# A two-layer hybrid block: the MLP's first stage with other places for the next layer's modulation, an earlier start of its second stage, and late row sums on GpSimd

## The chip, the cores and the metric

One core of one Trainium2 chip runs the whole program: TensorE (PE, with its weight loads PEld), VectorE (DVE), ScalarE (ACT), GpSimd (POOL), and SyncE (SP), which issues all DMAs of this part. The metric is the device time of one execution in microseconds; smaller is better.

## The reference

Two layers work on a latent sequence `x` of 1024 tokens and a context of 256 tokens, width 1024. Each layer makes six modulation vectors from a conditioning vector, runs a mixer (an mLSTM with windowed attention in layer 0, full grouped attention in layer 1), and then a squared-ReLU MLP:

```python
def sq_relu_mlp(h, w1, w2):
    return jnp.square(jax.nn.relu(h @ w1)) @ w2
...
mod_l = (jax.nn.silu(c) @ ada_w[layer] + ada_b[layer]).reshape(batch, 1, N_MOD, D_MODEL)
...
x = x + mod_l[:, :, 2] * y_l
x = x + mod_l[:, :, 5] * sq_relu_mlp(modulate(x, norm2_g[layer], mod_l, 3), mlp_w1[layer], mlp_w2[layer])
if not last:
    ctx = ctx + mod_c[:, :, 5] * sq_relu_mlp(modulate(ctx, norm2_g[layer], mod_c, 3), mlp_w1[layer], mlp_w2[layer])
```

`w1` is 1024 x 4096, `w2` 4096 x 1024, and `ada_w` 1024 x 6144 per layer. The context's MLP runs in layer 0 alone.

## The kernel before

All matrix products are split into a high and a low float32r part, and each becomes three matmuls: high by high, high by low, low by high. A split is one ACT instruction (the high part, L389) and one subtraction on POOL or DVE (the low part, L390).

The MLP has two stages, and both use a Strassen-like scheme with seven products in the place of eight. **First stage** (`mlp_hidden`): 16 pairs of 128 hidden features. `pair(b, A, nxt)` is one of them for b from 2 to 15 (pairs 0 and 1 are made in `start`). It runs the seven products in this order, twelve matmuls of 128x512 each, named here by their left operand: **11, S1, 12, S2, 22, S3, S4**. In layer 0 two `direct` products for the context stand among them, one after 12 and one after S3, 24 matmuls of 128x256 each. So a pair of layer 0 takes nine PSUM banks, one after the other out of seven that rotate (`psp.tags["A"]`): the bank that product 11 of a pair writes is the one of product 12 of the pair before. What empties a bank is ACT for 11 and the direct products, and DVE (`tt`, L635) for the six others; S2 and S3 are read twice. `finish` is a ReLU and a square on ACT (L592, L593) and a store (L595). From the finished tiles DVE makes column sums (`column_sums`, three additions of two SBUF tiles) and row sums (`row_sums`, two), each with a store to DRAM (`kept_sum`, L611); a pair's row sums run in the pair after, as `pending["row"]`. The first two pairs' sums are left for later: `late_load` reads their tiles back from DRAM after pairs 7 and 10, and `late_sums` makes all five sums in pairs 8 and 11.

After some products `pair` calls `step()`, which advances `nxt`: for most pairs this is `sums(b + 1, ...)`, which makes and splits the next pair's weight operands on POOL (L553, L390) and ACT (L389), a pair ahead. In pair 15 there is no next pair, and `nxt` is `ahead()`: it loads and splits the first three items (k = 0, 1, 2) of the **second stage** (`mlp_feed`, `mlp_out`), each of which has a weight part `a` and a hidden part `b` (`load_a`, `load_b`, L915; `split_a` with an addition on POOL, L960; `split_b`). The raw tiles of `a` lie in three places of the buffer F that the first stage's weights used; those of `b` lie in two more, which the scratch tile of `sums` and the filler's tiles below occupy until then. From the fourth item (k = 3) on, `feed.more()` loads into the buffers of the normalised input, which are free after the last product of the first stage, and splits on DVE.

In layer 0 a **filler** goes along: `ada_sums(1, block, ...)` makes the next layer's modulation, twelve blocks of 512 outputs. Each block loads eight chunks of `ada_w` (128x512, L204) and adds them up on DVE, scaled per partition (L211, L213); blocks 0 to 3 do it for latent and context, with two more instructions of 128x256 per chunk. Then 8 or 16 small matmuls against ones (L222) sum over the partitions, and DVE adds the bias (L225). It is a generator with three steps per block: chunks 0 to 3, chunks 4 to 7, and the matmuls with the bias. `fill(k)` in `pair` runs one step if b > k, at three places per pair.

Pairs 2 to 13 are ordered by the framework's planner: it works through the traced program with a cost model and can move an instruction of one engine ahead of others; program order is its priority. Pairs 14 and 15 stand in a `manual_schedule` block: there PE, DVE, ACT, POOL and SP keep the order in which the program is written. On every engine, and in SP's queue of DMA issues, an instruction that waits holds up all that stand behind it.

The second stage (L1037) takes per item 24 matmuls of 128x512 from four banks each of two output halves; items 0 and 1 are taken together, in four works of twelve: item 0, item 1, item 0, item 1.

Of the kernel before, what the change touches and what calls it, by code (L numbers as in the profile page):

```python
# [10 lines left out]
F32 = mybir.dt.float32  # L11
# [3 lines left out]
ALU = mybir.AluOpType  # L15
# [4 lines left out]
P = 128  # L20
# [76 lines left out]
class Kernel:  # L97
# [96 lines left out]
            nc.vector.tensor_tensor(dst[:, :, :, vv], src[:, :, :, vv], bias, op=ALU.add)  # L194
        yield

    def ada_sums(self, layer, block, streams, tp, psp, tag):


        nc, a = self.nc, self.a  # L200
        acc = [[tp.tile([P, n], F32, tag=f"acc{v}") for _ in range(512 // n)] for v, n in enumerate((512, 256)[:streams])]
        for k in range(ND):
            w = tp.tile([P, 512], F32, tag="raw")
            nc.sync.dma_start(w, a["ada_w"][layer, k * P : (k + 1) * P, block * 512 : block * 512 + 512])  # L204
            for v in range(streams):
                c = self.cs[:, k, v : v + 1]
                n = 512 // len(acc[v])
                for i, t in enumerate(acc[v]):
                    x = w[:, i * n : i * n + n]
                    if k == 0:  # L210
                        nc.vector.tensor_scalar(t, x, c, None, op0=ALU.mult)  # L211
                    else:
                        nc.vector.scalar_tensor_tensor(t, x, c, t, op0=ALU.mult, op1=ALU.add)  # L213
            if k % 4 == 3:
                yield
        pt = psp.tile(tag, "adapt")
        for v in range(streams):
            n = 4 // len(acc[v])
            for i in range(4):
                o = 8 * v + 2 * i  # L220
                t = acc[v][i // n][:, i % n * P : i % n * P + P]
                nc.tensor.matmul(pt[:, o : o + 2], t, self.ones[:, 0:2], start=True, stop=True)  # L222
        c0 = block * 4
        for v in range(streams):
            nc.vector.tensor_tensor(  # L225
                self.mod[layer][:, c0 : c0 + 4, v], pt[:, 8 * v : 8 * v + 8].rearrange("p (i e) -> p i e", e=2)[:, :, 0],
                self.v(V_AB + layer * 48 + c0, 4), op=ALU.add,
            )
        yield

    def ada_quarter(self, q, tp, psp):

# [273 lines left out]
    def mlp_hidden(self, layer, groups, hds, begin, slots, tp, feed, filler):  # L506
# [80 lines left out]
        def temp(n=512):  # L587
            return tp.tile([P, n], F32, tag="u")
# [20 lines left out]
        def kept_sum(b, i, o, p, q, how=ALU.add):  # L609
            tt(o, p, q, how)  # L610
            nc.sync.dma_start(part(b, i), o)  # L611

        def late_load(b):

            h = [temp() for _ in range(4)]
            for t, i in zip(h, (5, 7, 8, 2)):
                nc.sync.dma_start(t, part(b, i))

            def late_sums():
                column_sums(b, h[0], h[2], h[3])  # L620
                row_sums(b, h[0], h[1], h[3])

            return late_sums

# [2 lines left out]
            kept_sum(b, 0, temp(), h11, h22)  # L627
            kept_sum(b, 4, h21, h21, h22)

        def row_sums(b, h11, h12, h22):  # L630
            kept_sum(b, 6, temp(), h12, h22, ALU.subtract)
            kept_sum(b, 3, h12, h11, h12)

        def tt(o, p, q, how=ALU.add):
            nc.vector.tensor_tensor(o, p, q, op=how)  # L635
# [150 lines left out]
        def pair(b, A, nxt):  # L786
# [62 lines left out]
        def ahead():  # L849


            at = tp.tags["op"][1]
            w = W[slots[5]]
            tp.place("op", [parts[(at + i) % 10] for i in range(10)] + [w[:, :PG], w[:, PG:]])
            tp.place("raw", cuts(F, PG, 0, PG, 2 * PG))
            tp.place("b", cuts(F, PG, 5 * PG, 6 * PG))
            eng = nc.gpsimd
            if filler:
                yield
                yield  # L860
            for k in range(2):
                feed.load(k)
            feed.load_a(2)
            yield
            feed.split_a(0, eng)
            yield
            feed.split_b(0, eng)
            feed.load_b(2)
# [1440 lines left out]
def body(ctx: ExitStack, tc: tile.TileContext, a, out):  # L2309
# [68 lines left out]
    def filler(tp, psp, tag):  # L2378
        if not steps:

            steps.append(s for b in range(12) for s in k.ada_sums(1, b, 2 if b < 4 else 1, tp, psp, tag))
        return steps[0]

    def to_mixer1(g, psp, gap):
# [30 lines left out]
```

## Time and profile before

| | |
|---|---|
| median of 3 runs | 2825.57 us (2825.43 to 2827.79) |
| the profiled execution | 2826.91 us; its span from first to last instruction is 2825.1 us |
| PE busy | 2716.9 us (96%) |
| DVE, ACT, POOL busy | 1953.8 (69%), 1474.9 (52%), 1114.1 us (39%) |
| granted TensorE clock, mean | 0.986 |
| first stage, pairs 2 to 15: layer 0, layer 1 | about 840 to 1231 us, about 2238 to 2504 us |
| second stage begins: layer 0, layer 1 | about 1231 us, about 2504 us |

Times in the profile are microseconds from the first instruction. A busy PE is not PE at its peak, since a matmul's record overlaps the next one's; what tells a loss is idle time before a matmul and the granted clock. In a row of the timeline the bracket at the end is the idle time of that engine just before the instruction, and what ended it. In the view by stretches, each engine's column is its busy time in the stretch, with the number of instructions, and the last three columns are the granted clock, the DMA engines' busy share and the rate.

### The profile page before, as it was taken

How to read it: one execution, taken by the hardware profiler on the slowest of the kernel's cores; microseconds unless marked ns; L12 is line 12 of the kernel's file. 1: busy time of each engine (PE TensorE's matmuls, PEld its weight loads, DVE VectorE, ACT ScalarE, POOL GpSimd, SP SyncE). 2: the span in 40 equal slices, each digit the busy share in tenths (PEclk: the TensorE clock that was granted, in tenths of full speed). 3: DMA queues.
4: the chain of work that ended last, by engine and by line, in shares of the span. 5: the costliest groups of instructions: out<-in, count | busy, mean ns of one | idle time of the engine just before them, and what ended most of it. 6: DMA issues, size and time to landing. Idle time of an engine off the chain costs nothing.

```text
span 2825.1 us, 40958 instructions
## 1 busy us (share of the span) xinstructions
PE 2716.9 (96%) x14747; PEld 2303.2 (82%) x14747; DVE 1953.8 (69%) x3299; ACT 1474.9 (52%) x2611; POOL 1114.1 (39%) x741
## 2 busy tenths in 40 slices
PE   6899999999999999989999999999999999999999
PEld 3788888878788887868888889999988888878877
DVE  4645555578878877667778756888874667666676
ACT  4755554444664343334346646888865555444442
POOL 2421121111238565630001346777775398740000
PEclk9999999999999999999999999999999999999999
DMA  7222233442325567578856820000036155477674
GB/s 238 66 78 94 94 101 137 142 162 87 119 84 154 179 214 233 167 251 304 282 182 193 254 68 25 22 27 20 27 119 215 58 172 199 166 269 261 220 228 153
DMA packets 194661, 428.36 MB, mean 152 GB/s; under 512 B 21128, under 2 KB 47336, under 8 KB 194456
## 3 DMA queue, kind: packets, MB, share of 16 engines
q1 hardware_dynamic: 194456, 425.73, 45.7%
q8 instruction: 116, 1.90, 0.3%
q14 instruction: 89, 0.73, 0.1%
HBM read 322.90 MB, written 102.74 MB: 151 GB/s over the span
## 4 chain that ended last, share of the span: by engine, by line
PE 61%; DVE 12%; DMA 6%; issue 5%; ACT 3%; POOL 3%; SPq 0%; DVEq 0%; POOLq 0%; ACTq 0%
PE psum L1037 16%; PE psum L580 11%; PE psum L415 4%; PE psum L417 4%; PE psum L416 4%; PE psum L2003 4%; PE psum L2189 3%; PE psum L1133 3%; DMA hhiraw<-in_w 3%; PE psum L1909 3%; DVE F L635 2%; POOL W L390 2%; DVE W L390 2%; DVE x L213 1%; DVE F L213 1%
## 5 line engine op out<-in xcount | busy, mean ns | idle before, releaser
L390 POOL TENSOR_TENSOR W<-F,W 128x512 fp32r<-128x512 f32 (+2 forms) x323 | 518.0, 1619 | 546.9 <-ACT W L389 430.0
L1037 PE MATMUL psum<-W,W 128*128 128x512 f32 x2688 | 620.2, 393 | 14.9 <-POOL W L390 8.3
L1037 PEld LDWEIGHTS psum<-W,W 128*128 128x128 f32 x2688 | 507.1, 189 | 127.7 <-POOL W L390 10.1
L580 PE MATMUL psum<-hhi,W 128*128 128x512 f32 (+1 forms) x1600 | 450.1, 361 | 10.2 <-DVE x L635 8.3
L389 ACT ACTIVATE W<-F 128x512 fp32r<-128x512 f32 (+2 forms) x380 | 273.4, 739 | 263.8 <-POOL F L553 97.7
L580 PEld LDWEIGHTS psum<-hhi,W 128*128 128x128 f32 x1600 | 290.0, 192 | 56.8 <-DVE x L635 8.0
L580 PE MATMUL psum<-hlo,W 128*128 128x512 f32 (+1 forms) x800 | 287.9, 360 | 0.0
L389 ACT ACTIVATE W<-hhiraw 128x1024 fp32r<-128x1024 f32 x98 | 103.8, 1060 | 308.6 <-PE psum L1037 204.2
L415 PE MATMUL psum<-hhi,W 128*128 128x512 f32 (+1 forms) x624 | 233.4, 374 | 0.5 <-ACT F L1422 0.5
L417 PE MATMUL psum<-hhi,W 128*128 128x512 f32 (+1 forms) x624 | 227.0, 364 | 0.0
L416 PE MATMUL psum<-hlo,W 128*128 128x512 f32 (+1 forms) x624 | 226.6, 363 | 0.0
L553 POOL TENSOR_TENSOR F<-F 128x512 f32<-128x512 f32 x112 | 167.5, 1496 | 19.4 <-DMA F<-in_w 10.8
L960 DVE TENSOR_TENSOR hhiraw<-hhiraw 128x512 f32<-128x512 f32 x154 | 106.2, 701 | 98.2 <-DMA hhiraw<-in_w 97.4
L580 PEld LDWEIGHTS psum<-hlo,W 128*128 128x128 f32 x800 | 154.0, 192 | 21.6 <-issue 0.2
L390 DVE TENSOR_TENSOR W<-hhiraw,W 128x1024 fp32r<-128x1024 f32 x98 | 119.7, 1222 | 64.9 <-ACT W L389 63.6
L382 POOL TENSOR_TENSOR hlo<-F,hhi 128x512 fp32r<-128x512 f32 (+1 forms) x24 | 27.4, 1144 | 342.4 <-ACT F L373 342.4
L415 PEld LDWEIGHTS psum<-hhi,W 128*128 128x128 f32 x624 | 118.2, 189 | 21.0 <-ACT x L389 2.5
L416 PEld LDWEIGHTS psum<-hlo,W 128*128 128x128 f32 x624 | 118.4, 190 | 17.3 <-issue 2.2
L417 PEld LDWEIGHTS psum<-hhi,W 128*128 128x128 f32 x624 | 118.1, 189 | 17.0 <-issue 0.2
L390 DVE TENSOR_TENSOR W<-hloraw,W 128x1024 fp32r<-128x1024 f32 x98 | 119.6, 1220 | 6.8 <-ACT W L389 6.8
L592 ACT ACTIVATE F<-F 128x512 f32<-128x512 f32 x82 | 51.3, 626 | 139.5 <-DVE F L635 139.5
L580 PE MATMUL psum<-x,W 128*128 128x512 f32 x504 | 123.5, 389 | 0.0
(442 smaller groups left out, 6367.6 us busy)
## 6 DMA issues: line engine op xcount, KB each, us to landing
F<-in_w SPq DMA_DIRECT2D x104, 512.0 KB
hloraw<-hd SPq DMA_DIRECT2D x90, 512.0 KB
hhiraw<-in_w SPq DMA_DIRECT2D x72, 512.0 KB
hd<-F SPq DMA_DIRECT2D x142, 256.0 KB
hhiraw<-in_w SPq DMA_DIRECT2D x116, 256.0 KB
F<-in_ada_w SPq DMA_DIRECT2D x96, 256.0 KB
hd<-x SPq DMA_DIRECT2D x90, 256.0 KB
F<-in_win SPq DMA_DIRECT2D x33, 512.0 KB
```

What stands on the lines that cost most here:

```text
L389: nc.scalar.activation(hi, src, AF.Copy)
L390: eng.tensor_tensor(lo, src, hi.bitcast(F32), op=ALU.subtract)
L415: nc.tensor.matmul(ps, sh, mh, start=i == 0, stop=False)
L416: nc.tensor.matmul(ps, sh, ml, start=False, stop=False)
L417: nc.tensor.matmul(ps, sl, mh, start=False, stop=i == n - 1)
L553: add = lambda o, p, q, how: nc.gpsimd.tensor_tensor(o, p, q, op=how)
L580: nc.tensor.matmul(ps, w[i][:, p], B[j][k], start=first and j == 0 and m == 0, stop=last and j == 3 and m == 2)
L960: tt = lambda o, p, q, how: eng.tensor_tensor(o, p, q, op=how)
L1037: nc.tensor.matmul(bank(base + i), A[u][:, p], B[v], start=first and m == 0, stop=last and m == 2)
L1133: nc.tensor.matmul(bank(k), B[u][:, i * P : i * P + P], A[v][:, half], start=f == 0 and m == 0, stop=f == NFF - 1 and m == 2,)
L1909: nc.tensor.matmul(ps, s[:, c], m[:, j, t0 : t0 + QT], start=j == 0 and i == 0, stop=j == ND - 1 and i == 2)
L2003: nc.tensor.matmul(u.o[:, :QT], v[x], p[y], start=c == 0 and m == 0, stop=c == 2 * NB - 1 and m == 2)
```

## The change

Five edits, in both layers unless said otherwise:

1. `ada_sums` takes all twelve blocks in one generator and keeps up to three chunk loads ahead, also over the end of a step or of a block: `load()` runs before each chunk and again just before a step ends. The tiles are the same three as before.
2. The filler's steps move in `pair` (layer 0): the first two from around the reading of product 12 to behind the two readings of S2, the third from behind 22 to behind the readings of S3.
3. In `ahead`, layer 0 begins two steps earlier, and in both layers loads and splits are interleaved: loads of a0, b0, a1 after product 11; split a0 after S1; split b0 and the load of a2 after 12; the load of b1 and split a1 after S2; the load of b2 after 22; split b1 after S3; splits a2 and b2 after S4. Layer 1 loaded a0, b0, a1, b1 and a2 after product 11 before, and split a1 and b1 both after S3.
4. The raw places of `a` in the second stage begin with the third of the three.
5. `late_sums` makes its two row sums on POOL in the place of DVE: two instructions in pair 8 and two in pair 11 of each layer.

```diff
+    def ada_sums(self, layer, blocks, tp, psp, tag):
...
+        todo = deque((block, k) for block, _ in blocks for k in range(ND))
+        ready = deque()
+        def load():
+            while todo and len(ready) < 3:
+                block, k = todo.popleft()
+                ready.append(tp.tile([P, 512], F32, tag="raw"))
+                src = a["ada_w"][layer, k * P : (k + 1) * P, block * 512 : block * 512 + 512]
+                nc.sync.dma_start(ready[-1], src)
...
         for k in range(ND):
-            w = tp.tile([P, 512], F32, tag="raw")
-            nc.sync.dma_start(w, a["ada_w"][layer, k * P : (k + 1) * P, block * 512 : block * 512 + 512])
+                load()
+                w = ready.popleft()
...
-            if k % 4 == 3:
-                yield
+                if k % 4 == 3:
+                    load()
+                    yield
...
-                row_sums(b, h[0], h[1], h[3])
+                row_sums(b, h[0], h[1], h[3], nc.gpsimd)
...
             prod(ps, A["12"], B21)
-            fill(3)
             tt(h11, ps, t)
             finish(h11, h11, part(b, 5))
-            fill(2)
...
             prod(ps, A["S2"], T2)
             tt(v, ps, v)
             tt(t, ps, t)
+            fill(3)
+            fill(2)
             step()
             ps = bank()
             prod(ps, A["22"], T4)
             tt(t, t, ps, ALU.subtract)
-            fill(2)
             step()
             ps = bank()
             prod(ps, A["S3"], T3)
...
             finish(t, t)
             finish(h22, h22, part(b, 2))
+            fill(2)
...
-            tp.place("raw", cuts(F, PG, 0, PG, 2 * PG))
+            tp.place("raw", cuts(F, PG, 2 * PG, 0, PG))
...
-            if filler:
-                yield
-                yield
-            for k in range(2):
-                feed.load(k)
+            feed.load(0)
+            feed.load_a(1)
+            yield
+            feed.split_a(0, eng)
+            yield
+            feed.split_b(0, eng)
             feed.load_a(2)
             yield
-            feed.split_a(0, eng)
-            yield
-            feed.split_b(0, eng)
+            feed.load_b(1)
+            feed.split_a(1, eng)
+            yield
             feed.load_b(2)
             yield
-            if not filler:
-                yield
-                yield
-            for k in (1, 2):
-                feed.split_a(k, eng)
-                feed.split_b(k, eng)
-                yield
+            feed.split_b(1, eng)
+            yield
+            feed.split_a(2, eng)
+            feed.split_b(2, eng)
+            yield
```

More of the change, by code (lines that the diff above doesn't have):

```diff
@@ L195, in ada_steps @@
         yield
-    def ada_sums(self, layer, block, streams, tp, psp, tag):
+    def ada_sums(self, layer, blocks, tp, psp, tag):
         nc, a = self.nc, self.a
-        acc = [[tp.tile([P, n], F32, tag=f"acc{v}") for _ in range(512 // n)] for v, n in enumerate((512, 256)[:streams])]
-        for k in range(ND):
-            w = tp.tile([P, 512], F32, tag="raw")
-            nc.sync.dma_start(w, a["ada_w"][layer, k * P : (k + 1) * P, block * 512 : block * 512 + 512])
-            for v in range(streams):
[L206 to L213, printed above, removed]
-            if k % 4 == 3:
-                yield
[L216 to L228, printed above, removed]
-        yield
@@ new lines, in ada_sums @@
+        todo = deque((block, k) for block, _ in blocks for k in range(ND))
[6 more added lines that the diff above has]
+                nc.sync.dma_start(ready[-1], src)
+        for block, streams in blocks:
+            acc = [
+                [tp.tile([P, n], F32, tag=f"acc{v}") for _ in range(512 // n)]
+                for v, n in enumerate((512, 256)[:streams])
+            ]
+            for k in range(ND):
+                load()
+                w = ready.popleft()
+                for v in range(streams):
+                    c = self.cs[:, k, v : v + 1]
+                    n = 512 // len(acc[v])
+                    for i, t in enumerate(acc[v]):
+                        x = w[:, i * n : i * n + n]
+                        if k == 0:
+                            nc.vector.tensor_scalar(t, x, c, None, op0=ALU.mult)
+                        else:
+                            nc.vector.scalar_tensor_tensor(t, x, c, t, op0=ALU.mult, op1=ALU.add)
+                if k % 4 == 3:
+                    load()
+                    yield
+            pt = psp.tile(tag, "adapt")
+            for v in range(streams):
+                n = 4 // len(acc[v])
+                for i in range(4):
+                    o = 8 * v + 2 * i
+                    t = acc[v][i // n][:, i % n * P : i % n * P + P]
+                    nc.tensor.matmul(pt[:, o : o + 2], t, self.ones[:, 0:2], start=True, stop=True)
+            c0 = block * 4
+            for v in range(streams):
+                nc.vector.tensor_tensor(
+                    self.mod[layer][:, c0 : c0 + 4, v],
+                    pt[:, 8 * v : 8 * v + 8].rearrange("p (i e) -> p i e", e=2)[:, :, 0],
+                    self.v(V_AB + layer * 48 + c0, 4), op=ALU.add,
+                )
+            yield
@@ L607, in direct, with kept_sum @@
             job() if later is None else later.append(job)
-        def kept_sum(b, i, o, p, q, how=ALU.add):
-            tt(o, p, q, how)
+        def kept_sum(b, i, o, p, q, how=ALU.add, eng=nc.vector):
+            eng.tensor_tensor(o, p, q, op=how)
             nc.sync.dma_start(part(b, i), o)
@@ L628, in column_sums, with row_sums @@
             kept_sum(b, 4, h21, h21, h22)
-        def row_sums(b, h11, h12, h22):
-            kept_sum(b, 6, temp(), h12, h22, ALU.subtract)
-            kept_sum(b, 3, h12, h11, h12)
+        def row_sums(b, h11, h12, h22, eng=nc.vector):
+            kept_sum(b, 6, temp(), h12, h22, ALU.subtract, eng)
+            kept_sum(b, 3, h12, h11, h12, ALU.add, eng)
         def tt(o, p, q, how=ALU.add):
@@ L2379, in filler @@
         if not steps:
-            steps.append(s for b in range(12) for s in k.ada_sums(1, b, 2 if b < 4 else 1, tp, psp, tag))
+            steps.append(k.ada_sums(1, [(b, 2 if b < 4 else 1) for b in range(12)], tp, psp, tag))
         return steps[0]
```

2 lines of the change are left out of this document (1 added, 1 removed).

## The prediction

> **What bounds the kernel now.** I read the page first, then the view by stretches, then what TensorE waited for, and last the timelines around the waits. The page says that PE is nearly always busy, so only idle PE time and a lowered clock can be won back. The stretches say where these lie: the first stage's pairs in layer 0, its end in layer 0, the same pairs in layer 1, its end there.
>
> ```profile
> PE 2716.9 (96%) x14747; PEld 2303.2 (82%) x14747; DVE 1953.8 (69%) x3299; ACT 1474.9 (52%) x2611; POOL 1114.1 (39%) x741
> ```
>
> ```profile
> core 0: us, PE busy (x) PEld busy (x) DVE busy (x) ACT busy (x) POOL busy (x), PEclk, DMA share, GB/s
> 840.00:1231.00 391.00, 375.49 (x1982) 324.02 (x1980) 302.23 (x367) 150.06 (x294) 243.28 (x164) 0.97 0.57 186
> 1231.00:1260.00 29.00, 20.16 (x73) 15.47 (x74) 14.11 (x10) 12.89 (x17) 19.68 (x9) 0.82 0.79 270
> 2195.00:2504.00 309.00, 309.00 (x1363) 255.63 (x1362) 208.66 (x238) 159.13 (x273) 230.92 (x158) 1.00 0.45 152
> 2504.00:2520.00 16.00, 12.94 (x44) 9.69 (x44) 9.12 (x6) 7.25 (x9) 11.54 (x5) 0.79 0.92 302
> ```
>
> Layer 0's pairs lose 391.0 - 375.5 = 15.5 us idle and at most 0.03 x 391 = 11.7 us to the clock: 27 us. The end of that stage loses 8.8 + 0.18 x 29 = 14 us, layer 1's end 3.1 + 0.21 x 16 = 6.4 us, and layer 1's pairs nothing. So at most 47 us are to be had. From the same rows a 128x512 matmul takes 309.0 / 1363 = 0.227 us, a product of twelve 2.7 us.
>
> The next view is of the first stage's matmuls: what ended their idle time, and the waits themselves.
>
> ```profile
>   DVE x L635: 16.3, 10
> 955.38 1.87 PE L222 MATMUL psum<-ones,F 128*128 128x2 f32 x8 [3.58 <-DVE F L213]
> 1034.90 0.51 PE L580 MATMUL psum<-hhi,W 128*128 128x512 f32 x1 [3.12 <-DVE x L635]
> 1118.70 0.79 PE L580 MATMUL psum<-hhi,W 128*128 128x512 f32 x1 [3.08 <-DVE x L635]
> 1206.11 0.47 PE L580 MATMUL psum<-hhi,W 128*128 128x512 f32 x1 [1.73 <-DVE x L635]
> 1211.18 1.05 PE L222 MATMUL psum<-ones,F 128*128 128x2 f32 x8 [2.06 <-DVE F L213]
> 940.00:960.00 20.00, 16.42 (x77) 14.19 (x76) 18.81 (x31) 7.44 (x16) 9.20 (x6) 0.85 0.59 187
> ```
>
> Five waits make 13.6 of the 15.5 us, and DVE ends all of them: twice the modulation's matmuls wait for its last chunk, three times a product waits for DVE to empty a bank. POOL ends none. The first cost a clock of 0.85 over 20 us, 3 us more. This is DVE's queue before the second wait, in pair 8:
>
> ```profile
> 1024.63 1.77 DVE L635 TENSOR_TENSOR F<-x,F 128x512 f32<-128x512 f32 x1
> 1026.43 1.67 DVE L635 TENSOR_TENSOR x<-x,x 128x512 f32<-128x512 f32 x1
> ...
> 1028.70 0.84 DVE L211 TENSOR_SCALAR F<-F,cs 128x512 f32<-128x512 f32 x1
> 1029.57 3.35 DVE L213 SCALAR_TENSOR_TENSOR F<-F,cs 128x512 f32<-128x512 f32 x2
> 1032.84 0.68 DVE L635 TENSOR_TENSOR F<-x,x 128x512 f32<-128x512 f32 x1
> 1034.17 0.68 DVE L635 TENSOR_TENSOR x<-psum,F 128x512 f32<-128x512 f32 x1
> ```
>
> The last row empties product 12's bank, which product 11 of pair 9 awaits. Late sums (the first two rows, which I take for the two row sums by their place in the code) and three chunks of the filler stand ahead of it. Last, what DVE itself waits for in these pairs, and what a chunk costs it:
>
> ```profile
> DVE F L635 <- DMA hd<-F: 17.8, 8, 3.2
> DVE F L635 <- ACT x L593: 13.2, 8, 4.3
> DVE x L635 <- ACT F L593: 10.5, 11, 3.0
> DVE F L213 <- DMA F<-in_ada_w: 6.7, 12, 1.4
> DVE F L211 <- DMA F<-in_ada_w: 4.7, 1, 4.7
> L213 DVE SCALAR_TENSOR_TENSOR F<-F,cs 128x512 f32<-128x512 f32 x82 | 91.1, 1111 | 8.0 <-DMA F<-in_ada_w 6.7
> L213 DVE SCALAR_TENSOR_TENSOR x<-F,cs,x 128x256 f32<-128x256 f32 x56 | 44.1, 823 | 0.0
> ```
>
> A block costs DVE 8 x 1.11 = 8.9 us, one with two streams 16 x 0.82 more, 22 us. DVE is busy 302 of 391 us and idle 89; without the 27 us lost the stage lasts 364, so DVE may then idle only 62. The whole gain needs DVE shorter by 27 us; that is the measure for the next part.
>
> **The change part by part.** *Late row sums to POOL.* In pairs 8 and 11 DVE loses 1.77 + 1.67 = 3.4 us each, against waits of 3.12 and 3.08. POOL gains two instructions each, some 1.6 us apiece like its others; it is busy 243 of 391 us and ends no wait of a product. It could still be held in its queue by a store that must land before a temporary is free (up to 3.2 us in the rows above), and the operand splits with it: a loss of 0 to 3.2 us each, taken as 0, since operands are made a pair ahead. In layer 1 the same four instructions meet a POOL with 78 idle of 309 us and a PE that never waits: 0. With the clock behind both waits (some 4 us) up to 10 us are to be won, none if the pressure on DVE only moves; I take 8.
>
> One row argues against this move: the same addition takes DVE 0.68 us at 1032.84 and 1.77 at 1024.63. The Trainium skill (SBUF — State Buffer, on the port pair that DVE and GpSimd share) says that a DVE instruction with two SBUF inputs and a GpSimd instruction that reads SBUF exclude each other, and the second waits until the first is done. The two durations agree with it. By it each moved sum could still hold DVE's column sums for one instruction, and the 8 us would be about 3; the sum below keeps 8.
>
> *The filler's steps at other products (layer 0).* The work is the same; its place in DVE's queue is not. The steps now stand behind the readings of 12, of S2 and of S3, so banks are emptied first. The third step falls between S3's `finish` on ACT and the column sums that wait for it, so it can fill the 24 us that DVE waits for L593 in the two ACT rows above; I count on half, 12 us. The modulation's matmuls stand one direct product and S2 later on PE: 2.7 + about 3 = 5.6 us more for the last chunk, against 3.58 us missing in pair 6; two to four readings of 0.68 us go ahead of it on DVE. So that wait should go; what is late next is the emptying of 12's bank in pair 6 or 7. I take 5 of the 3.6 + 3 us and the slower tail behind them; bounds 0 and 8.
>
> *Three chunks in flight.* In the planned pairs SP already issues a chunk as soon as a buffer is free (DVE waits 1.4 us at most), so nothing there. In pairs 14 and 15, in written order, it does:
>
> ```profile
> 1198.93 0.75 DVE L211 TENSOR_SCALAR F<-F,cs 128x512 f32<-128x512 f32 x1 [4.72 <-DMA F<-in_ada_w]
> 1210.37 0.75 DVE L213 SCALAR_TENSOR_TENSOR F<-F,cs 128x512 f32<-128x512 f32 x1 [1.37 <-DMA F<-in_ada_w]
> 1200.00:1220.00 20.00, 16.20 (x80) 13.67 (x78) 14.59 (x18) 6.19 (x12) 7.91 (x6) 0.91 0.42 133
> ```
>
> The loads stood behind stores in SP's queue. Issued a step earlier they spare DVE 4.72 + 1.37 = 6.1 us, more than the 1.73 + 2.06 us that PE waits here; with 0.09 x 20 = 1.8 us of clock that is 5.6 us; I take 5 (0 to 5.6).
>
> The clock needs a word. Here waits of 1.73 and 2.06 us cost a clock of 0.91. The Trainium skill (TensorE: Matmul & The Clock Gate, Part 1) has the clock halved after an idle window of about 3.4 us; this row shows shorter waits doing it. By that rule the waits that remain would cost nothing more, by this row about 1.8 us for each 4.
>
> Together the pairs of layer 0 give 8 + 5 + 5 = 18 us (bounds 3 and 27). DVE's account: 3.4 x 2 + 6.1 + 12 = 25 us shorter, near the 27 that the whole would need.
>
> *The second stage's start, layer 0.* SP, POOL, ACT and PE at the change of stages:
>
> ```profile
> 1226.72 0.90 SPq L915 DMA_DIRECT2D F<-in_w  x2
> 1231.28 1.26 POOL L960 TENSOR_TENSOR F<-F 128x512 f32<-128x512 f32 x1 [11.15 <-DMA F<-in_w]
> 1232.57 2.00 ACT L389 ACTIVATE W<-F 128x1024 fp32r<-128x1024 f32 x2 [6.29 <-POOL F L960]
> 1234.63 0.79 PE L1037 MATMUL psum<-W,W 128*128 128x512 f32 x1 [4.09 <-ACT W L389]
> 1238.88 6.55 PE L1037 MATMUL psum<-W,W 128*128 128x512 f32 x17 [3.46 <-POOL W L390]
> 1247.82 0.88 SPq L915 DMA_DIRECT2D hhiraw<-in_w  x2
> ```
>
> Item 0's load is issued at 1226.72, too late, and ACT's `finish` work stands behind its split for 6.29 us. Now a0, b0 and a1 go out right behind pair 14's column-sum stores, two products and a direct product earlier and past the row sums: over 8 us. The splits of a0, b0, a1 then lie beside pair 15's products. b1's load has to await the modulation's matmuls, whose accumulators lie under it, now behind S2; its split is due only after the direct product behind S3, so that costs nothing. But item 3 is late next: its loads at 1247.82 stand behind the row-sum stores of pair 15. PE wants it 6 x 2.7 = 16 us after the last product, near 1247 on this clock; the loads move up by some 9 us, between ACT's wait of 6.3 and POOL's of 11.2, to about 1239, and with landing, addition and splits (an estimate from item 0's rows: 1231.28 - 1226.72 = 4.6 to land, 1.3 for the addition, 2.0 on ACT, then half of POOL's 5.14 for two in layer 1's rows below, in all 10.5) item 3 is ready at 1249, 2 to 5 us late. So of 14 us I take 8, bounds 4 and 14.
>
> *Layer 1's end.* Nothing makes a0 earlier here: its load already stood after product 11.
>
> ```profile
> 2502.66 1.30 POOL L960 TENSOR_TENSOR F<-F 128x512 f32<-128x512 f32 x1
> 2505.12 1.99 ACT L389 ACTIVATE W<-F 128x1024 fp32r<-128x1024 f32 x2
> 2506.24 5.14 POOL L390 TENSOR_TENSOR W<-F,W 128x1024 fp32r<-128x1024 f32 x2 [2.28 <-ACT W L389]
> 2511.44 2.08 PE L1037 MATMUL psum<-W,W 128*128 128x512 f32 x4 [3.06 <-POOL W L390]
> ```
>
> a1's high part can start on ACT at 2504.0 instead of 2505.1, but S3's four `finish` instructions (2.5 us) now stand behind it and ahead of b1's, which then comes at 2507.6; POOL makes b1's low part from about 2508.7, as before. The wait of 3.06 us stays: 0, bounds -3 (column sums delayed by 2.5 us, and item 3's loads with them) and +6.
>
> **Sum.** 18 + 8 + 0 = 26 us: 2826.9 - 26 = 2800.9 us by the profiled execution, which stands 1.3 us above the median shown (2825.57), so 2800 us.
>
> **The rivals.** *The waits only move.* Wherever PE runs ahead, DVE is late at the next bank, since its own waits for stores (hd, 17.8 us) and its work are the same. For it: DVE ends every wait. Against it: 6.1 + 6.8 us leave DVE's queue for certain. Then pairs give 5 and the start 6 us: 2826.9 - 11 - 1.3 = 2815 us. *It doesn't do what it says.* The planner puts the filler's chunks where its model sees DVE idle, wherever they are written, and item 3 takes back the start's gain: bounds 3 and 0, 2823 us. *Slower: the modulation's matmuls wait at their new place.* If chunks 4 to 7, now behind S3's readings, end over 5.6 us later than before (plus what margin they have), PE waits at each of the twelve blocks. Two us each are 24; less the start's 8, that is 2826.9 + 16 - 1.3 = 2842 us. For it: with two streams a step is 4 x 1.11 + 8 x 0.82 = 11 us, and DVE is behind. Against it: only two to four readings go ahead of it newly.
>
> **The numbers.** The forecast has 0.62 (its own range 2790 to 2811), moving waits 0.17, no effect 0.11, slower 0.10. Changes under 0.2%, 5.7 us, can't be told from none. Faster is 0.62 + 0.17 less a little of its edge: 0.78; same 0.12; slower 0.10. Left out of the range from 2787 to 2823 are the slower rival and the edges, 2 in 10.
>
> **What the profile would show.** Right: no wait of over 1 us before products of pairs 9 and 12; L222 starting without idle time in pair 6; no DVE wait for in_ada_w over 1.5 us near pair 14; item 0's loads over 8 us before the last product ends; DVE's idle time for L593 halved. Wrong: PE waits on DVE L635 in other pairs, L222 waits on L213 behind S2, or L1037 waits for item 3.

## The result and the profile after

| | before | after |
|---|---|---|
| median | 2826.55 us (2823.82 to 2835.06, 22 runs) | 2832.33 us (2824.16 to 2837.47, 22 runs) |
| ratio to before, 95% interval | | 1.0015 (1.0008 to 1.0021): 4.2 us slower |
| the profiled execution | 2826.91 us | 2836.66 us, span 2834.9 us |

Not 26 us faster, but 4 us slower. Single executions of one kernel differ by 10 us: the first matmul of the first stage, behind code that the change doesn't touch, starts at 785.0 us in the one trace and at 788.9 in the other. So times are compared below by ratios of many runs, and traces by their waits.

The view by stretches, cut at the ends of the stages as before (1241 for 1231, 2518 for 2504):

```profile
core 0: us, PE busy (x) PEld busy (x) DVE busy (x) ACT busy (x) POOL busy (x), PEclk, DMA share, GB/s
840.00:1241.00 401.00, 383.39 (x2015) 328.95 (x2014) 303.19 (x365) 153.06 (x296) 253.54 (x170) 0.97 0.55 181
1241.00:1270.00 29.00, 21.63 (x71) 16.34 (x72) 16.81 (x18) 14.65 (x21) 15.17 (x7) 0.76 0.98 337
2207.00:2518.00 311.00, 311.00 (x1372) 257.25 (x1371) 209.37 (x236) 160.40 (x275) 238.19 (x163) 1.00 0.46 156
2518.00:2534.00 16.00, 14.93 (x65) 11.78 (x64) 11.53 (x10) 6.27 (x8) 9.07 (x4) 1.00 0.86 302
```

Layer 0's pairs lose 401.0 - 383.4 = 17.6 us where they lost 15.5. The start of layer 0's second stage still loses 7.4 us (8.8 before) and runs at a clock of 0.76 (0.82 before). Layer 1's start loses 1.1 us at full clock, where it lost 3.1 at 0.79. What PE waited for from 840 to 1270 us, and what DVE waited for from 840 to 1241 (total, times, longest):

```profile
PE psum L238 <- DVE F L228: 13.9, 8, 3.5
PE psum L1053 <- ACT W L406: 2.7, 1, 2.7
PE psum L1053 <- ACT F L609: 2.5, 1, 2.5
PE psum L1053 <- POOL W L407: 2.4, 2, 1.9
PE psum L238 <- DVE x L228: 2.3, 4, 0.8
PE psum L597 <- DVE x L652: 1.2, 2, 0.8
```

```profile
DVE F L228 <- DMA F<-in_ada_w: 30.4, 10, 5.2
...
DVE F L627 <- ACT x L610: 4.5, 3, 1.8
DVE x L627 <- ACT F L610: 4.4, 2, 3.0
```

(L238 is now the modulation's matmul, L228 the scaled sum, L210 the chunk's load, L652 `tt`, L627 the kept sums, L609 and L610 `finish`, L406 and L407 the split, L562 the load of w1, L1053 the second stage.) The waits for banks of products, 8.3 us before by this view, are down to 1.2. DVE's two waits for `finish` that the prediction counted, 13.2 and 10.5 us, are down to 4.5 and 4.4. The view of the kernel before has a third of the same size that the prediction left out:

```profile
DVE F L635 <- ACT F L593: 12.4, 7, 4.3
```

With it and a small one of 2.6 us, DVE waited 38.7 us for `finish` before; in the changed kernel all such rows together are 9.7 us (4.5, 4.4 and 0.8). But the modulation's matmuls wait 16.2 us at eight blocks (5.6 before, at two), and DVE waits 30.4 us for chunks (11.4 before). One such wait, in pair 10, with POOL's, SP's and DVE's rows:

```profile
1064.82 6.21 POOL L407 TENSOR_TENSOR W<-F,W 128x512 fp32r<-128x512 f32 x4 [0.89 <-ACT W L406]
1069.81 0.33 SPq L562 DMA_DIRECT2D F<-in_w  x1
1070.23 5.12 SPq L210 DMA_DIRECT2D F<-in_ada_w  x4
1064.74 0.48 DVE L226 TENSOR_SCALAR F<-F,cs 128x512 f32<-128x512 f32 x1
1065.25 3.38 DVE L228 SCALAR_TENSOR_TENSOR F<-F,cs 128x512 f32<-128x512 f32 x2
1074.24 0.75 DVE L228 SCALAR_TENSOR_TENSOR F<-F,cs 128x512 f32<-128x512 f32 x1 [5.02 <-DMA F<-in_ada_w]
```

Chunk 0 frees its buffer at 1065.2 us, so chunk 3's load could go then. It goes at 1070.23: in SP's queue it stands behind a store that waits for ACT until 1066.5, and then behind a load of `w1`, whose buffer POOL's split frees only at 1069.8. Here the order of DMA issues sets DVE's pace. It does not always set PE's: the next matmuls of the modulation, at 1084.3 us, start without idle time. Of DVE's four waits of over 5 us for a chunk (at 1074, 1103, 1161 and 1191 us), two are followed by a wait of these matmuls (1.85 and 1.99 us) and two by none, and PE's longest, 3.53 us at 1056.9, follows a wait for a chunk of only 1.82. So the trace alone doesn't show that the loads are the loss; the runs below test it.

### The profile page after: what moved, and what is told of

It reads as the page before. It is cut to its first block, busy times and chain, and to the rows that moved or that the text cites. A ratio compares the mean times of both kernels' runs of the same rounds, so it can differ in the third digit from the quotient of the medians.

```text
span 2834.9 us, 40967 instructions
## 1 busy us (share of the span) xinstructions
PE 2723.0 (96%) x14747; PEld 2302.7 (81%) x14747; DVE 1950.8 (69%) x3291; ACT 1476.0 (52%) x2611; POOL 1125.3 (40%) x749
## 4 chain that ended last, share of the span: by engine, by line
PE 61%; DVE 12%; DMA 8%; issue 5%; POOL 3%; ACT 2%; SPq 0%; DVEq 0%; POOLq 0%; ACTq 0%
PE psum L1053 14%; PE psum L597 12%; PE psum L432 4%; PE psum L433 4%; PE psum L434 4%; PE psum L2019 4%; DMA hhiraw<-in_w 4%; PE psum L2205 3%; PE psum L1149 3%; PE psum L1925 3%; DVE W L407 2%; POOL W L407 2%; DVE x L228 1%; DMA F<-in_ada_w 1%; DVE F L627 1%
## 5 line engine op out<-in xcount | busy, mean ns | idle before, releaser
L407 POOL TENSOR_TENSOR W<-F,W 128x512 fp32r<-128x512 f32 (+2 forms) x323 | 517.6, 1617 | 554.3 <-ACT W L406 436.4
L1053 PE MATMUL psum<-W,W 128*128 128x512 f32 x2688 | 621.6, 393 | 14.1 <-DVE W L407 5.5
L1053 PEld LDWEIGHTS psum<-W,W 128*128 128x128 f32 x2688 | 506.0, 189 | 129.4 <-DVE W L407 12.9
L406 ACT ACTIVATE W<-F 128x512 fp32r<-128x512 f32 (+2 forms) x380 | 273.1, 739 | 259.2 <-POOL F L570 109.1
L406 ACT ACTIVATE W<-hhiraw 128x1024 fp32r<-128x1024 f32 x98 | 104.0, 1061 | 318.9 <-PE psum L1053 240.7
L407 DVE TENSOR_TENSOR W<-hhiraw,W 128x1024 fp32r<-128x1024 f32 x98 | 119.7, 1222 | 67.3 <-ACT W L406 64.9
L597 PE MATMUL psum<-x,W 128*128 128x512 f32 x504 | 131.5, 408 | 0.0
L609 ACT ACTIVATE F<-F 128x512 f32<-128x512 f32 x82 | 51.3, 626 | 139.4 <-DVE F L652 139.4
L407 DVE TENSOR_TENSOR W<-hloraw,W 128x1024 fp32r<-128x1024 f32 x98 | 119.5, 1219 | 0.1
```

Of the source, the lines that this page charges most:

```text
L406: nc.scalar.activation(hi, src, AF.Copy)
L407: eng.tensor_tensor(lo, src, hi.bitcast(F32), op=ALU.subtract)
L597: nc.tensor.matmul(ps, w[i][:, p], B[j][k], start=first and j == 0 and m == 0, stop=last and j == 3 and m == 2)
L1053: nc.tensor.matmul(bank(base + i), A[u][:, p], B[v], start=first and m == 0, stop=last and m == 2)
```

## The experiments

Each ratio is against the kernel before, run beside it on the same chip. 0.001 is 2.8 us. With intervals of about 0.001 to each side, two of these ratios are clearly different from about 0.0015 on, some 4 us (an estimate from the intervals).

| filler's places | chunk loads from SP | from ACT | only three loaded |
|---|---|---|---|
| old (12, 12, 22) | 0.9980 (0.9971 to 0.9990) | 0.9994 (0.9984 to 1.0005) | 0.9985 (0.9974 to 0.9995) |
| mixed (12, 12, S3) | 0.9973 (0.9963 to 0.9984) | 0.9985 (0.9976 to 0.9994) | |
| new (S2, S2, S3) | 1.0015 (the changed kernel) | 0.9971 (0.9959 to 0.9983) | 0.9908 (0.9892 to 0.9923) |

**Old places.** `fill(3)` and `fill(2)` back around the reading of 12, the other `fill(2)` behind 22's.

> The changed kernel with the filler's three steps back at their old places in the pair (around the reading of 12 and behind 22); the other four edits stay. Theory A (the move ate the gain): in the changed kernel PE waits 16.2 us in front of or inside the modulation's matmuls behind S2, 5.6 us before the change; with the old places these waits fall to 6 us or less, while the banks of pairs 9 and 12 stay free of waits over 1 us, since the late row sums are on GpSimd: 10 to 15 us faster than the changed kernel, some 2819 us. Theory B (PE waits for DVE in one place or another, because DVE's work is the bound): the waits only change their matmuls, and the time stays within 3 us of the changed kernel's 2832.

2822.5 us, 9.9 us under the changed kernel by the ratios: the moved steps alone cost more than the change lost. But the bank waits of pairs 9 and 12 came back, with the row sums on GpSimd:

```profile
PE psum L597 <- DVE x L652: 8.3, 2, 4.7
PE psum L238 <- DVE F L228: 5.1, 3, 4.7
```

**Late row sums back on DVE**, once in the changed kernel, once with the old places:

```diff
-                row_sums(b, h[0], h[1], h[3], nc.gpsimd)
+                row_sums(b, h[0], h[1], h[3])
```

> The changed kernel with the late row sums back on VectorE. Theory A: the two 3 us waits for a bank in pairs 9 and 12 come back, with their slow clock: 4 to 8 us slower than the changed kernel, some 2838 us. Theory B (the move only shifts waits): within 3 us. Theory C (the additions on GpSimd hold up VectorE at the port that both use): 2 to 4 us faster, some 2829 us.

> The changed kernel with the old places of the filler and the late row sums on VectorE: the three chunks in flight and the new order ahead of the second stage stay. Against the kernel with the old filler places alone (2822.5 us), which still waits 3.61 and 4.67 us for the banks in pairs 9 and 12. Theory A (the row sums on GpSimd free nothing on VectorE, which then runs at half its pace beside them): within 2 us, with bank waits of 3 to 5 us in both. Theory B (the row sums on GpSimd win what the prediction said): 4 to 8 us slower, some 2828 us.

1.0014 (1.0004 to 1.0025) beside the changed kernel's 1.0015, and 0.9972 (0.9963 to 0.9982) beside 0.9980: nothing, in either. With DVE's row sums and the old places the banks are awaited 1.29 and 3.60 us, less than with GpSimd's.

**The old order ahead of the second stage**, in the changed kernel and with the old places (`ahead` as in the kernel before).

> The changed kernel with the old order of loads and splits ahead of the second stage, in both layers, and the old raw places. Theory A: the new order brings 1.7 us at the change of stages in layer 0 and 3.9 us in layer 1, so the old one is 4 to 7 us slower than the changed kernel, some 2838 us; the wait of 3 us before the second stage of layer 1 comes back. Theory B (layer 0's second stage pays for the early items with 2.3 us of late waits near 1440 to 1492 us, and the clock stays low there all the same): 1 to 4 us slower, all of it in layer 1. Theory C (the difference in layer 1 is scatter of one execution): within 2 us.

> The changed kernel with the old places of the filler and the old order ahead of the second stage, in both layers: of the change, the three chunks in flight and the late row sums on GpSimd stay. Against the kernel with the old filler places alone (2822.5 us). Theory A: the new order gives some 2 us at the change of stages in layer 0 and 2 to 4 us in layer 1, so this kernel is 3 to 6 us slower, some 2827 us, and has the wait of 3 us with its slow clock before the second stage of layer 1. Theory B: only scatter, within 2 us of 2822.5.

The first is no clean test: with the filler at its new places, b1's load is written ahead of the last block's matmuls and overwrites the sums that they read, so that block of the modulation is wrong (this is read from the written order); PE idled 15.3 us at the start of the second stage, and it took 2851.8 us. The second is clean: 2826.4 us, ratio 0.9997 (0.9988 to 1.0006), so the new order is worth 0.0017, 4.8 us, in both layers together; that is little more than the two intervals allow to tell. The second stage's first matmuls in layer 0, and the wait in layer 1, in this kernel:

```profile
1232.07 0.80 PE L1053 MATMUL psum<-W,W 128*128 128x512 f32 x1 [5.22 <-ACT W L406]
1236.32 4.95 PE L1053 MATMUL psum<-W,W 128*128 128x512 f32 x12 [3.45 <-POOL W L407]
1244.31 2.08 PE L1053 MATMUL psum<-W,W 128*128 128x512 f32 x4 [3.05 <-POOL W L407]
...
2509.30 3.00 PE L1053 MATMUL psum<-W,W 128*128 128x512 f32 x8 [3.19 <-POOL W L407]
```

With the new order they were, in the kernel with the old places:

```profile
1229.08 0.49 PE L1053 MATMUL psum<-W,W 128*128 128x512 f32 x1 [1.11 <-ACT W L406]
1231.51 1.58 PE L1053 MATMUL psum<-W,W 128*128 128x512 f32 x5 [1.93 <-POOL W L407]
1236.48 3.24 PE L1053 MATMUL psum<-W,W 128*128 128x512 f32 x7 [3.39 <-ACT F L609]
1240.32 4.84 PE L1053 MATMUL psum<-W,W 128*128 128x512 f32 x20 [0.60 <-POOL W L407]
...
2504.93 3.25 PE L1053 MATMUL psum<-W,W 128*128 128x512 f32 x13 [1.09 <-POOL W L407]
```

11.7 us of waits became 7.0 in layer 0, and 3.19 became 1.09 in layer 1. What is late next is ACT's `finish` of a direct product, whose bank the second stage needs.

**One chunk in flight** (`len(ready) < 1`, no `load()` at a step's end).

> The changed kernel with one chunk of the modulation's weights loaded at its own use, as before, in the place of up to three ahead. Theory A: VectorE waits some 6 us more for chunks in pairs 14 and 15, PE 2 to 5 us of it: 2 to 5 us slower than the changed kernel, some 2836 us. Theory B (three loads at once stand in SyncE's queue ahead of the stores and operand loads, and this slows the planned pairs): 2 to 5 us faster.

1.0036 (1.0026 to 1.0047), 5.9 us slower than the changed kernel: at the new places three in flight are worth what was foreseen. With the old places and the old order, three chunks and the row sums together gave 0.8 us (0.9997), so there they are worth nothing that this can tell.

**Chunks 4 to 7 back behind 22**, and **the matmuls behind the reading of 12** instead of ahead of it: two ways of changing DVE's order while PE keeps its own.

> The changed kernel with one of the filler's three steps, chunks 4 to 7, back behind the reading of 22, a product earlier than behind S3's readings; the matmuls stay behind S2, and PE's order is that of the changed kernel. Theory A (the waits of the modulation's matmuls come from chunks 4 to 7 standing too late): these waits fall from 16 us to 6 us or less, and the time to 2820 to 2825 us. Theory B (VectorE is behind as a whole, and its order changes only which matmul waits): the waits move to banks of products, and the time is within 3 us of 2832.

> The changed kernel with the filler at its old places, except that the modulation's matmuls and bias stand behind the reading of product 12's bank in the written order, not ahead of it. PE's order is that of the kernel with the old places; VectorE's differs in a few rows. Theory A (the bank waits of 3.61 and 4.67 us in pairs 9 and 12 come from three chunks that stand ahead of that reading): both waits fall below 1.5 us, and the time by 6 to 10 us below 2822.5, some 2815 us. Theory B (sums at half pace make the reading late whatever the chunks do): waits of 2 us or more stay there, and the time is within 3 us of 2822.5.

1.0026 (1.0015 to 1.0037) and 0.9982 (0.9973 to 0.9991): no gain in either, and theory A missed in both. In the first the waits became waits for banks, and DVE's for chunks stayed (28.4 us):

```profile
PE psum L597 <- DVE x L652: 7.2, 3, 3.9
PE psum L238 <- DVE F L228: 6.6, 3, 3.1
PE psum L597 <- DVE F L652: 4.7, 2, 3.6
```

In the second, waits of 2.38 and 4.68 us for the banks stayed in pairs 9 and 12. So neither of these two orders on DVE was the cause; something else made DVE late in both.

**No loads, mixed places, less work, another queue.** The four that tell the loads from DVE's work:

```diff
-                nc.sync.dma_start(ready[-1], src)
+                if block == 0 and k < 3: nc.sync.dma_start(ready[-1], src)   # no loads
+                nc.scalar.dma_start(ready[-1], src)                          # ScalarE's queue
-                for v in range(streams):
+                for v in range(streams if k == 0 else 1):                    # less work
```

> The changed kernel with only the first three chunks of the modulation's weights loaded and their data used again for all the others: 93 loads less in SyncE's queue, the same work on VectorE and the same order of PE in the first stage of layer 0. (The second layer's modulation is then made from the wrong weights.) Theory A (the moved steps ask for chunks while SyncE's queue stands behind a weight load that waits for GpSimd; VectorE waits 30.4 us for chunks, 11.4 before the change): these waits go, and the first stage of layer 0 (451.8 us from first to last matmul in the changed kernel, 445.6 before) shortens to 443 us or less, the time to 2822 or less. Theory B (VectorE's work is the bound, and a wait for a chunk is only where its idle time is put): 450 us or more there, the time within 3 us of 2832.

> The changed kernel with the modulation's matmuls and chunks 0 to 3 at their old place at product 12, and only chunks 4 to 7 at the new one behind S3's readings: the steps stand five products apart instead of two and seven. PE's order is that of the kernel with all steps at the old places. Theory A (two steps close together outrun three buffers and the loads): VectorE's waits for chunks stay under 12 us, and the time is that of the old places, 2822.5, or up to 4 us less, since readings of 22 come earlier. Theory B (chunks behind S3 come too late for the matmuls of the next pair, wherever those stand): waits of the matmuls of 10 us or more and 2828 us or more.

> The changed kernel without the context's share of chunks 1 to 7 in blocks 0 to 3: 56 instructions of 128x256 less on VectorE, some 44 us of its work in pairs 3 to 7. (The context's modulation in the second layer is then wrong.) Loads and matmuls stay. Theory A (in the pairs with two streams VectorE's work is the limit, in the later ones the loads): the waits at 962 and 994 us (2.3 and 2.5 us with those inside) go, those from 1026 us on stay: 3 to 8 us faster than the changed kernel. Theory B (loads are the limit in all pairs): within 2 us of 2832.

> The changed kernel with the loads of the modulation's chunks issued by ScalarE's queue in the place of SyncE's; all else as it is. Theory A (in SyncE's queue the chunks stand behind weight loads and stores that wait): VectorE's waits for chunks fall from 30.4 us to 12 us or less and the time to 2820 to 2826 us. Theory B (a load that waits for a free buffer now holds up ScalarE's work, the splits and finishes): VectorE and PE wait for ScalarE in its place, and the time is 2832 us or more.

Without the loads 2804.2 us: 0.0107, 30 us, under the changed kernel, with the same instructions on DVE. PE's waits for DVE from 840 to 1216 us, and the stretch:

```profile
PE psum L597 <- DVE x L652: 3.2, 1, 3.2
PE psum L597 <- DVE F L652: 2.0, 4, 0.7
PE psum L238 <- DVE F L228: 0.7, 2, 0.4
```

```profile
840.00:1216.00 376.00, 370.13 (x2015) 320.56 (x2014) 300.44 (x369) 157.28 (x304) 266.12 (x173) 1.00 0.41 134
```

DVE is as busy as in the changed kernel (300 against 303 us), in 25 us less, and the clock is 1.00. So DVE's work was not what bound this stage. Less work (0.9996, 0.9988 to 1.0005) won 5.4 us, though DVE then waited 57 us for chunks, and of the two waits that were to go the one at 990 us grew to 3.98. Mixed places (2822.6 us) are as good as the old ones, and DVE waits 12.5 us for chunks there. The loads from ScalarE's queue, with the same bytes and PE's order untouched, won 0.0044, 12.4 us. In pair 10 the load for which DVE waited 5.02 us:

```profile
1063.43 0.33 ACTq L210 DMA_DIRECT2D F<-in_ada_w  x1
1066.59 3.22 DVE L228 SCALAR_TENSOR_TENSOR F<-F,cs 128x512 f32<-128x512 f32 x2 [2.09 <-DMA F<-in_ada_w]
```

The wait is 2.09. But the number expected for the view missed: DVE's waits for chunks are still 31.6 us in all, now 20 short ones (3.1 at most). Only 3.6 us of the matmuls' 16.2 are left, but PE's waits for banks of products rose from 1.2 to 9.4 us. Why the same total of DVE's waits costs PE less is not shown. Two other causes can be looked at in the traces. The chunks' loads, which wait in SP's queue for their buffers (91 us in all in the changed kernel), could have held up the stores: but DVE's waits for stores (`hd`) rose with ScalarE's queue, from 41.5 to 46.7 us. And DVE's sums of a chunk ran faster with it (990 ns against 1079 on average for 128x512, 658 against 787 for 128x256), some 14.5 us of DVE's time for the 82 and 56 instructions, an estimate; how much of the 12.4 us that made is not known. The price of this queue is in the trace too: a load that waits for its buffer now holds up ACT's own work, one split by 4.32 us at 1068.5.

**What is left: the read-back.** In the kernel with the chunks on ScalarE's queue DVE waits 8.2 and 8.0 us for the late tiles' loads (2.6 and 3.8 in the changed kernel), and PE 3.49 and 5.18 us behind them in pairs 9 and 12. Leaving out the loads (`if not filler:` ahead of `late_load`'s DMA), and the old and mixed places with ScalarE's queue:

> The kernel with the filler's steps at their old places (2822.5 us), without layer 0's eight loads that read tiles of pairs 0 and 1 back from DRAM; the late sums run on what their tiles hold (so these hidden sums are wrong), with the same work on VectorE and GpSimd. Theory A (the bank of product 12 is emptied late in pairs 8 and 11 since late column sums ahead of that reading wait for the read-back, whose loads stand behind stores in SyncE's queue): the waits of 3.61 and 4.67 us before products of pairs 9 and 12 fall below 1 us, and the time by 8 to 12 us to some 2813. Theory B (the additions and chunks at half pace beside GpSimd make it late): waits of 2 us or more stay, and the time is within 3 us of 2822.5.

> The changed kernel with the chunks' loads on ScalarE's queue (2821 us) and without layer 0's eight loads of late tiles; the late sums run on what their tiles hold (so these hidden sums are wrong). Theory A (the bank waits of 3.49 and 5.18 us at 1037 and 1122 us come from the read-back, for which VectorE waits 8.2 and 8.0 us): they go, with their slow clock: 2808 to 2812 us. Theory B: waits of 2 us or more stay there, and the time is within 3 us of 2821.

> The kernel with the filler's steps at their old places, with the chunks' loads issued by ScalarE's queue. Theory A (the places matter only through SyncE's queue): about 2821 us, as with the changed places and ScalarE's queue. Theory B (the old places are better by themselves): 2815 us or less. Theory C (with the old places VectorE hardly waits for chunks, 8.7 us, so the other queue only adds waits to ScalarE): 2823 to 2828 us.

> The kernel with the mixed places (matmuls and chunks 0 to 3 at product 12, chunks 4 to 7 behind S3), with the chunks' loads issued by ScalarE's queue. Theory A: about 2821 us, places matter only through the queue. Theory B (VectorE's waits for chunks, 12.5 us there, go, and with them the waits of the matmuls at 959, 990 and 1217 us, 7.5 us in all): 2813 to 2818 us.

With the old places the read-back is worth nothing (0.9987, 0.9976 to 0.9998), though the two waits at 1037 and 1123 us went: others of 0.8 to 2.6 us took their place. With the new places and the chunks out of SP's queue it is worth 0.0024, 7 us (0.9947, 0.9934 to 0.9960), but theory A holds only by half: PE's wait in pair 12 fell to 1.51 us, the one in pair 9 stayed, at 3.79, with no read-back to wait for. The other queue does nothing for the old and mixed places: there DVE waited little for chunks (8.7 and 12.5 us), and some 15 us with ScalarE's queue.

**The last two:** the old places without loads, and the changed kernel with the chunks and the read-back from ScalarE's queue (`nc.scalar.dma_start(t, part(b, i))`, sixteen loads, eight in each layer), which leaves nothing out.

> The changed kernel with the filler's steps at their old places, and only the first three chunks of the modulation's weights loaded, their data used again for the others. (The second layer's modulation is then made from the wrong weights.) To be held against the new places without loads, 2804 us. Theory A (the new places empty banks earlier, as predicted, and only the loads spoil them): bank waits of 3 to 5 us in pairs 9 and 12 stay with the old places, and the time is 2810 to 2818 us. Theory B (the places do not matter where no chunk is awaited): 2801 to 2807 us. Theory C (with the old places hardly a chunk was awaited, so leaving the loads out gives nothing): 2820 us or more.

> The changed kernel with the chunks' loads and the loads that read late tiles back both on ScalarE's queue; against the chunks' loads alone there (2821 us) PE, VectorE and GpSimd keep their order. Theory A (the read-back is late since its loads stand behind stores in SyncE's queue): VectorE's waits of 8.2 and 8.0 us for it fall below 3 us, PE's of 3.49 and 5.18 us in pairs 9 and 12 below 1.5, and the time to 2810 to 2815 us. Theory B (it is late since its buffers come free late, whichever queue issues it): the waits stay, the time is within 3 us of 2821. Theory C (ScalarE's work now stands behind loads that wait): slower than 2824.

The old places without loads take 2822.8 us, as with them. So the same loads cost 30 us at the new places and nothing at the old ones; the traffic that they leave free wins nothing by itself there. With no chunk to await, the new places are 0.0077, 22 us, better than the old. PE's waits with the old places and no loads, from 840 to 1228 us:

```profile
PE psum L597 <- DVE x L652: 10.9, 3, 5.3
PE psum L238 <- DVE F L228: 5.5, 2, 4.5
```

The last kernel takes 2808.8 us, ratio 0.9937 (0.9923 to 0.9950): 17.8 us faster than before and 22 us faster than the change. PE's waits up to 1260 us, DVE's for the late tiles, and the stretch:

```profile
PE psum L597 <- DVE x L652: 4.2, 2, 2.9
...
PE psum L238 <- DVE F L228: 1.0, 1, 1.0
```

```profile
DVE F L627 <- DMA x<-hd: 4.2, 1, 4.2
DVE F L627 <- DMA F<-hd: 3.3, 1, 3.3
```

```profile
840.00:1218.00 378.00, 371.88 (x2000) 321.06 (x1998) 271.74 (x363) 153.86 (x296) 240.75 (x170) 0.99 0.58 192
```

It lies 0.0034, 9.6 us, under the kernel with only the chunks on ACT's queue, where leaving layer 0's read-back out gave 7; the two can't be told apart. Theory A fits best, though its numbers for the waits were too low: DVE's for the read-back went from 8 to 4.2 and 3.3, not below 3, and PE's two to 2.90 and 1.32. The 8 us from here to the kernel without loads (0.9937 to 0.9908) stay open: DVE's 30.7 us of waits for chunks, which remain, and the traffic were not told apart at the new places.

## Why the prediction was wrong, step by step

By the ratios the path from before to after is: chunks and row sums -0.8 us (0.9997), the order ahead of the second stage -4.8 (0.9980), the filler's places +9.9 (1.0015), in all +4.2, against 8 + 5 + 5 + 8 = 26 us foreseen. The step that failed is the price of the moved steps: it counted what the banks' readings gain and took 0 as its worst case, and it left out that a moved step moves its loads to another place in SP's queue. The bounds said for the pairs, 3 and 27, are not the sum of the parts' bounds either, which is 0 to 23.6.

- **Late row sums to POOL, 8 us: 0.** "None if the pressure on DVE only moves" was the lower bound, and it is what happened. The two sums left DVE's queue, but what stands between them and 12's reading got slower or waited. In the kernel with the old places and the row sums on GpSimd, the two late column sums ahead of that reading took 1.58 and 1.64 us, where they took 0.68 and 0.69 before, and the instruction for chunk 0 took 1.42 in place of 0.84:

```profile
1033.43 1.58 DVE L627 TENSOR_TENSOR F<-x,x 128x512 f32<-128x512 f32 x1
1035.05 1.64 DVE L627 TENSOR_TENSOR x<-x,F 128x512 f32<-128x512 f32 x1
1036.61 0.68 DVE L652 TENSOR_TENSOR x<-psum,F 128x512 f32<-128x512 f32 x1
```

  A wait for a store ahead of them was 3.98 us (1.99 before), and in pair 11 DVE waited 2.17 us for the read-back, which was not in my account. The paragraph of the prediction that argued against the move, about 3 us in the place of 8, was nearer.
- **Three chunks in flight, 5 us: 5.9 at the new places, about nothing at the old ones.** The size was right where the steps had moved. The sentence that failed is the one before it: "In the planned pairs SP already issues a chunk as soon as a buffer is free". That was read from DVE's waits of 1.4 us at the old places, which show that loads came in time there, not that SP's queue was free. Moved past a product or two, the steps ask for loads while SP's queue stands behind other issues (a store and `w1` in the case shown), and the waits grew to 5 us.
- **The filler's steps, 5 us gained: 9.9 lost.** The mechanism that I counted on is in the trace: bank waits 8.3 to 1.2 us, DVE's waits for `finish` 38.7 to 9.7 (I said half, of the 24 us in two of the rows). Without loads the places alone are worth 22 us. What I put at nothing is the moved step's own loads and the queue in which they stand: with them the same places lose 9.9 us.
- **The slower rival** had the right place, L238 behind S2, and the wrong reason: readings ahead of the chunks. I gave it 0.10 since only two to four readings go ahead; without the loads 0.7 us of these waits are left, so it was the loads, and 10.6 us of waits more (16.2 - 5.6), not 24.
- **The second stage's start, 8 us in layer 0 and 0 in layer 1: 4.8 in both together.** In layer 0 item 0 was early (its first load goes at 1192 us), but b0's split stood on ACT behind the `finish` of product 12, whose bank DVE read only at 1239.8, and item 1's behind POOL:

```profile
1239.76 1.89 DVE L652 TENSOR_TENSOR x<-psum,x 128x512 f32<-128x512 f32 x3 [2.24 <-DMA hd<-x]
1240.48 0.63 ACT L609 ACTIVATE x<-x 128x512 f32<-128x512 f32 x1 [7.73 <-DVE x L652]
1242.40 1.04 ACT L406 ACTIVATE W<-F 128x1024 fp32r<-128x1024 f32 x1
1243.49 0.50 PE L1053 MATMUL psum<-W,W 128*128 128x512 f32 x1 [2.70 <-ACT W L406]
1250.88 3.35 PE L1053 MATMUL psum<-W,W 128*128 128x512 f32 x7 [2.46 <-ACT F L609]
```

  Item 3, which I had late next, ends no wait there. In layer 1 I put a1's high part at the stage's end and b1's 3.2 us behind the last product. But a1's addition is done in time for its high part to run at 2513.51, 4 us ahead of the second stage's first matmul, so S3's `finish` is not held up by it; the rows below have b1's high part 0.6 us behind that matmul, and the wait fell from 3.06 to 1.07 us, with no slow clock behind it:

```profile
2517.46 3.31 PE L1053 MATMUL psum<-W,W 128*128 128x512 f32 x13
2521.84 8.50 PE L1053 MATMUL psum<-W,W 128*128 128x512 f32 x36 [1.07 <-POOL W L407]
...
2518.05 1.04 ACT L406 ACTIVATE W<-F 128x1024 fp32r<-128x1024 f32 x1
```

Of the five signs that were named, three came true: no wait of over 1 us before products of pairs 9 and 12, item 0's loads early, and DVE's waits for `finish` down by more than half. Two did not: the modulation's matmuls in pair 6 still waited (1.11 us, then 0.35 and 0.80), and DVE waited up to 5.23 us for chunks near pair 14. The range ended at 2823 us; the median of 2832 lies on the side of the slower rival, at a quarter of its loss (4 of 16 us).

## What to carry to other kernels

When a step moves, move its loads in your account too: look up what stands ahead of them in the issuing queue at the new place and what that waits for. A wait for a load that is short today only says that the load is in time at today's place. If one engine issues all DMAs, loads with a deadline can go from another engine's queue, and that is a cheap first experiment: here two lines were worth 22 us against the change. At the old places, where loads came in time, the same queue won nothing (0.9980 with SP, 0.9994 with ACT).

## What the runs showed of the hardware

The queue that issues a load mattered, with its bytes unchanged: the 96 loads of 256 KB moved from SP's to ACT's queue gave 12.4 us, the read-back's sixteen 9.6 more. The Trainium skill (DMA: Bandwidth & Descriptors, Issuing engines are not separate DMA queues) has it that starting DMAs on several engines only saves the time it takes to start them. Here starting one took 0.33 us, 32 us for the 96 (an estimate), but in the case shown the load was late by 5 us because issues ahead of it waited for ACT and POOL. So the wait of the issues ahead has to be counted too; how much of the 12.4 us is which was not separated.

Waits of one length slow the clock in one place and not in another. The stretch around a wait of 1.99 us of the modulation's matmuls in the changed kernel, the only one of over 1 us in it:

```profile
1195.00:1215.00 20.00, 18.01 (x89) 15.05 (x88) 12.49 (x15) 6.39 (x14) 8.85 (x6) 0.91 0.46 156
```

Right behind this wait stand eight matmuls of 128x2, another 1.05 us. Ahead of a full product, stretches of 20 us around waits of 2.36 us (the old places with the old order) and 3.20 us (the new places without loads) kept a clock of 1.00, while one of 2.90 us (the last kernel) had 0.91; the wait of 1.07 us in layer 1 left it at 1.00. The Trainium skill (TensorE: Matmul & The Clock Gate, Part 1) names an idle window of about 3.4 us. Waits of 1.99 and 2.90 us are less, so by their length alone the runs differ from it; whether the small matmuls count as idle was not tested.

Why DVE's sums of a chunk ran faster with ACT's queue is open. Less overlap with POOL's additions would explain it, but that was not tested.
